# FoX heads of a hybrid decoder: reciprocal row sums on the outputs, by way of DRAM, instead of on the probabilities

## The chip, the cores and the metric

The kernel runs on one core of a Trainium2 chip. The metric is device time in microseconds (us) of one execution, the median of several runs; lower is better. Engines in the profile: PE is TensorE (PEld its weight loads), DVE is VectorE, ACT is ScalarE, POOL is GpSimd, SP is SyncE, which issues most of the transfers.

## The reference

Two layers, each a feed-forward half step, a token mixer and a second feed-forward half step, for 512 tokens of width 1024 in float32. The mixer has 8 forgetting-attention (FoX) heads of width 64 and 4 differential heads. What matters here are the FoX heads:

```
s_f = einsum('bhqd,bhkd->bhqk', qf, k_f) * scale_f
s_f = s_f + cf[..., :, None] - cum_f[..., None, :]
s_f = where(causal, s_f, -inf)
p_f = softmax(s_f, axis=-1)
o_f = einsum('bhqk,bhkd->bhqd', p_f, v_f)
...
return concatenate([o_f, o_d], axis=-1) @ w_out
```

Softmax divides each row of exponentials by its sum. That factor depends on the query alone, so it may stand on the probabilities or on the output `o_f`.

## The kernel before

Every float32 matrix product is made from parts: an operand is split into a rounded high part (ACT) and the rest (DVE), and each product is two or three matmuls (`mm3`, L392 to L394). Weights stream from DRAM into `raw` tiles (issued by SP at L101) and are split into `wg` tiles; L83 and L84 are the two halves of a split, wherever it is called.

In the mixer the twelve heads are units 0 to 11, four differential and then eight FoX heads, and each has four query blocks of 128 rows. A loop over steps does, at step s, the softmax of block s mod 4 of unit s div 4 (`softmax_step`), the transposes of the probabilities of a unit about five steps earlier (`trans_step`, L878, evicted and split at L887 and L888), and the product with the values one step after that (`pv_step`, L917 and L918 for FoX). Between them `fill_to` puts other matmuls, by a table of targets: input projections, gates, values, and the early part of the output projection (`out_early`). When that filler runs short the FoX steps follow each other closely. `out_rest` finishes the output projection: it loads and splits the last block of W_out (rows 3 of eight, L1022) into tile G3, and its matmuls need the output of the last FoX pair.

This is the order in which the code asks for work. The framework under it then orders each engine's instructions by its own estimate of when they can start, and puts in the waits; each engine, and each queue of transfers, then runs strictly in that order.

A FoX block: scores into PSUM; L864 on DVE adds the forget term and finds the row's extreme; L866 on ACT takes the exponential in place and sums the row; L867 on DVE takes the reciprocal of the sum (128x1); L868 on ACT multiplies the block by it. The outputs of two heads are stacked as 128 rows (64 per head) by 512 queries in `fo["u"]` (L947 on ACT, L948 on DVE), and `split_o` (L899, L900) splits that for the output projection.

Probabilities, the pair's output and the rows' tiles lie in two tiles `pg` of 2048 columns, one for even and one for odd units. They occupy the buffers G3 and G4, which before and after the mixer hold weights:

```
pg = [home(f"G{3 + i}", [P, 2048], F32, f"pg{i}") for i in range(2)]
PR = {3: 0, 2: 512, 1: 896, 0: 1152}
...
def pm_tile():
    return pg[nxt("pm", 2)][:, 1280:1792]
```

The forget term of a head comes the same way as the new factors will: `cum_d` in DRAM is read back broadcast over all partitions (L861).

Of the kernel before, what the change touches and what calls it, by code (L numbers as in the profile page):

```python
# [8 lines left out]
F32 = mybir.dt.float32  # L9
F32R = mybir.dt.float32r  # L10
BF16 = mybir.dt.bfloat16
AF = mybir.ActivationFunctionType
ALU = mybir.AluOpType
AX = mybir.AxisListType

P = 128
S = 512
# [5 lines left out]
FOX_H = 8  # L23
DIFF_H = 4
NB = S // P
# [22 lines left out]
def rf(t):  # L48
    return t.bitcast(F32)
# [3 lines left out]
def trunk(ctx, tc, xT, x, gains, gain_row, w_gu, w_dn, w_in, w_ff, w_out, fbias, lams, subln, consts, rope, out):  # L53
    nc = tc.nc
    act, dve, pool, pe, sp = nc.scalar, nc.vector, nc.gpsimd, nc.tensor, nc.sync
# [3 lines left out]
    sm = ctx.enter_context(tc.tile_pool(name="sm", bufs=4))  # L59
    ps = ctx.enter_context(tc.tile_pool(name="ps", bufs=1, space=bass.MemoryType.PSUM))  # L60
    dram = ctx.enter_context(tc.tile_pool(name="dram", bufs=2, space=bass.MemoryType.DRAM))
# [7 lines left out]
    def psum(tag, name=None):  # L69
        return ps.tile([P, S], F32, tag=tag, name=name or f"ps_{tag}", bufs=3 if tag == "a" else 5)  # L70

    def home(tag, shape, dt, name):
        return sb.tile(shape, dt, tag=tag, name=name, bufs=1)

    def t_tile(shape, dt, name, i=None):
        return home(f"t{nxt('t', 6) if i is None else i}", shape, dt, name)
# [143 lines left out]
    for n in range(2 * DEPTH):  # L220
        l = n // 2
        if n % 2 == 1:
            for i in range(24 + len(OUT_K)):
                k = OUT_K[i - 24] if i >= 24 else None
                tag = MIX[i % 3] if i < 24 else None if k >= 4 else MIX[(i - 28) % 3]
# [361 lines left out]
    def mixer(l, n_next, mid):  # L587
# [11 lines left out]
        pg = [home(f"G{3 + i}", [P, 2048], F32, f"pg{i}") for i in range(2)]  # L599
        PR = {3: 0, 2: 512, 1: 896, 0: 1152}  # L600

        def pr_tile(u, qb):
            w = (qb + 1) * P
            return pg[u % 2][:, PR[qb]:PR[qb] + w]

        def pm_tile():
            return pg[nxt("pm", 2)][:, 1280:1792]

        def pair():
            t = home(f"s{nxt('pair', 3)}", [P, 2, S], F32R, "pair")  # L610
            return t[:, 0], t[:, 1]
# [3 lines left out]
        def y_pair(i):  # L615
            return ys[i // 4][:, i % 4], ys[i // 4][:, 4 + i % 4]
# [206 lines left out]
        def scores(q1, kk, m, qb, masked):  # L823
            n = (qb + 1) * P
            w = max(n, 256)
            p = psum("b")
            lq = q1[m][:, qb * P:n]
            pe.matmul(p[:, 0:w], lq, kk[m][:, 0, 0:w], start=True, stop=False)
            pe.matmul(p[:, 0:w], lq, kk[m][:, 1, 0:w], start=False, stop=not masked)
            if masked:  # L830
                pe.matmul(p[:, qb * P:n], identb, maskb, start=False, stop=True)
            return p

        cbs = {}

        def softmax_step(u, qb):
            kind, h = units[u]
            n = (qb + 1) * P
            st = sm.tile([P, 6], F32, tag="st", name="st", bufs=6)
            if kind == "d":  # L840
                q1, kk = qk[("d", h)]
                pm = []
                for m in range(2):
                    p = scores(q1, kk, m, qb, False)
                    e = pr_tile(u, qb) if m == 0 else pm_tile()
                    dve.tensor_tensor_reduce(out=e[:, 0:n], in0=p[:, 0:n], in1=maskw[:, S - n:S], op0=ALU.add,
                                             op1=ALU.min, scale=1.0, scalar=3.0e38, accum_out=st[:, m:m + 1])
                    act.activation(out=e[:, 0:n], in_=e[:, 0:n], func=AF.Exp, scale=-1.0, bias=st[:, m:m + 1],
                                   accum_out=st[:, 2 + m:3 + m])
                    pm.append(e)  # L850
                dve.reciprocal(out=st[:, 4:6], in_=st[:, 2:4])
                dve.tensor_tensor(out=st[:, 5:6], in0=st[:, 5:6], in1=nlam, op=ALU.mult)
                act.mul(out=pm[1][:, 0:n], in_=pm[1][:, 0:n], mul=st[:, 5:6])
                dve.scalar_tensor_tensor(out=pm[0], in0=pm[0], scalar=st[:, 4:5], in1=pm[1][:, 0:n],
                                         op0=ALU.mult, op1=ALU.add)
                probs[u].append(pm[0])
            else:
                q1, kk = qk[("f", h // 2)]
                if qb == 0:
                    cbs[h] = rope_t[h % 2]  # L860
                    sp.dma_start(out=cbs[h], in_=cum_d[h:h + 1, :].partition_broadcast(P))  # L861
                p = scores(q1, kk, h % 2, qb, True)
                e = pr_tile(u, qb)
                dve.tensor_tensor_reduce(out=e, in0=p[:, 0:n], in1=cbs[h][:, 0:n], op0=ALU.add, op1=ALU.min,  # L864
                                         scale=1.0, scalar=3.0e38, accum_out=st[:, 0:1])
                act.activation(out=e, in_=e, func=AF.Exp, scale=-1.0, bias=st[:, 0:1], accum_out=st[:, 2:3])  # L866
                dve.reciprocal(out=st[:, 4:5], in_=st[:, 2:3])  # L867
                act.mul(out=e, in_=e, mul=st[:, 4:5])  # L868
                probs[u].append(e)

        pts = {}

# [22 lines left out]
        fo = {}  # L895

        def split_o(i, u):
            oh, ol = y_pair(i)
            act.copy(out=oh, in_=u)  # L899
            dve.tensor_tensor(out=ol, in0=u, in1=rf(oh), op=ALU.subtract)  # L900
            ovt[i] = (oh, ol)

        def pv_step(u, kb):
            kind, h = units[u]
            if kb == 0:
                po_[u] = psum("b")
            po = po_[u]
            th, tl, cols = pts.pop((u, kb))
            hs = slice(h * P, (h + 1) * P)
            if kind == "d":  # L910
                vh, vl = vd[kb]
                pe.matmul(po[:, cols], vh[:, hs], th, start=kb == 0, stop=False)
                pe.matmul(po[:, cols], vl[:, hs], th, start=False, stop=False)
                pe.matmul(po[:, cols], vh[:, hs], tl, start=False, stop=kb == NB - 1)
            else:
                v = vf[kb][:, hs]
                pe.matmul(po[:, cols], v, th, start=kb == 0, stop=False)  # L917
                pe.matmul(po[:, cols], v, tl, start=False, stop=kb == NB - 1)  # L918
            if kb < NB - 1:
                return  # L920
            po_.pop(u)
            if kind == "d":
                o = os_[h // 2][:, h % 2]
                act.copy(out=o, in_=po)
                sq = t_tile([P, S], F32, "osq")
                act.activation(out=sq, in_=po, func=AF.Square)
                sh_, sl_ = pair()
                act.copy(out=sh_, in_=sq)
                dve.tensor_tensor(out=sl_, in0=sq, in1=rf(sh_), op=ALU.subtract)
                ov[h] = o  # L930

                def stats():
                    pq = psum("b")
                    pe.matmul(pq[0:32], ones[:, 0:32], sh_, start=True, stop=False)
                    pe.matmul(pq[0:32], ones[:, 0:32], sl_, start=False, stop=True)
                    act.activation(out=vv[32 * h:32 * h + 32], in_=pq[0:32], func=AF.Identity, scale=1.0 / P,
                                   bias=eps_t[0:32])
                    if h == DIFF_H - 1:
                        diff_norm()
                later.append(stats)  # L940
            else:
                if h % 2 == 0:
                    fo["u"] = pm_tile()
                own = slice(64 * (h % 2), 64 * (h % 2) + 64)
                oth = slice(64 - 64 * (h % 2), P - 64 * (h % 2))
                t = t_tile([P, S], F32, "fot")
                act.copy(out=t[own], in_=po[oth])  # L947
                dve.tensor_tensor(out=fo["u"][own], in0=po[own], in1=t[own], op=ALU.add)  # L948
                if h % 2 == 1:
                    split_o(h // 2, fo["u"])  # L950

        later = []
# [135 lines left out]
        for s in range(4 * len(units) + 5 + LAG):  # L1088
            u, i = divmod(s, 4)

            def pace(j):
                a = target[min(u, len(target) - 1)]
                b = target[min(u + 1, len(target) - 1)]
                fill_to(a + (b - a) * (3 * i + j) / 12)
            now, later[:] = list(later[:1]), later[1:]
            v, kb = divmod(s - 4 - LAG, 4)
            if 0 <= v < len(units):
                trans_step(v, kb)
            pace(1)
            if u < len(units):  # L1100
                softmax_step(u, i)
            pace(2)
            for f in now:
                f()
            v, kb = divmod(s - 5 - LAG, 4)
            if 0 <= v < len(units):
                pv_step(v, kb)
            pace(3)
# [250 lines left out]
```

## Time and profile before

| | |
|---|---|
| median of 3 runs | 1883.84 us (1880.58 to 1884.79) |
| profiled execution, its own time | 1882.77 us |
| its span, first to last instruction | 1880.5 us |
| mean granted TensorE clock | 0.992 |
| FoX softmax, layer 0 and layer 1 | about 481 to 578 us and 1405 to 1503 us |
| feed-forward after the mixer of layer 0, first matmul | 616.11 us |

How to read the lines further on. The page gives, for each engine, busy us, share of the span and instructions. A row of a stretch gives start and end, its length, then for each engine busy us and the number of instructions, then the granted TensorE clock, the busy share of the 16 transfer engines and GB/s. A row with ACT or DVE alone counts only one source line, named in the text. A row of waits reads: engine, tile and line that waited, `<-` what ended the wait, us in total, times, longest. A row of instructions in time reads: start, duration, engine, line, operation, output `<-` inputs, shape, and in brackets the idle time before it with what ended it. A row of groups gives busy us and mean ns of one. A row of transfers ends with the size and the median us from issue to landing.

### The profile page before, as it was taken

Reading aid. Unit: us, or ns where it says so; the run is one execution under the profiler, and the core shown is the slowest. Engines: PE = TensorE matmul, PEld = TensorE weight load, DVE = VectorE, ACT = ScalarE, POOL = GpSimd, SP = SyncE. Lnnn points to the kernel's source line nnn. Section 1 sums busy time; section 2 is a strip of 40 time slices with the busy share of each in tenths; the row PEclk is TensorE's granted clock in tenths of the full one; section 3 lists DMA queues with packets and bytes.
Section 4 is the critical chain, followed back from the end, with each engine's and each line's share of the span. In section 5 each row is a group of like instructions: output and inputs, shape, how many; then the busy total and the mean of one; then the engine's idle time right before and its main releaser. Section 6 shows DMA issues by size and latency. Waiting matters only on the chain.

```text
span 1880.5 us, 24723 instructions
## 1 busy us (share of the span) xinstructions
PE 1837.3 (98%) x8814; PEld 1511.3 (80%) x8814; DVE 1626.0 (86%) x2538; ACT 1139.3 (61%) x1797; POOL 131.1 (7%) x155
## 2 busy tenths in 40 slices
PE   8999999999999999999999999999999999999997
PEld 6788888787877889888878988887788788888886
DVE  8799989878685989899998989997786869998988
ACT  6565546556785755565485555555577957455564
POOL 2001000000000000001001001000000000000101
PEclk8999999999999999999999999999999999999999
DMA  9677675144336676676647667643333367757842
GB/s 303 190 202 196 166 198 157 59 133 122 94 108 190 182 197 175 162 209 186 169 145 208 183 168 190 169 132 112 112 112 103 111 176 195 208 150 186 223 113 89
DMA packets 95818, 304.86 MB, mean 162 GB/s; under 512 B 12600, under 2 KB 15160, under 8 KB 95696
## 3 DMA queue, kind: packets, MB, share of 16 engines
q1 hardware_dynamic: 74960, 232.68, 36.7%
q0 software_dynamic: 19440, 68.69, 20.8%
q10 hardware_dynamic: 1296, 1.93, 0.3%
q8 instruction: 69, 1.13, 0.2%
q14 instruction: 53, 0.43, 0.1%
HBM read 288.50 MB, written 2.16 MB: 155 GB/s over the span
## 4 chain that ended last, share of the span: by engine, by line
PE 82%; DVE 10%; ACT 5%; DMA 2%; issue 1%; SPq 0%; DVEq 0%; ACTq 0%
PE ps_c L392 12%; PE ps_c L393 12%; PE ps_c L394 12%; PE ps L394 9%; PE ps L392 9%; PE ps L393 9%; PE ps_a L392 3%; PE ps_a L393 3%; PE ps_a L394 3%; DVE wg L84 2%; PE ps_t L494 2%; DVE x L523 1%; ACT pg L866 1%; PE ps_b L878 1%; ACT wg L83 1%
## 5 line engine op out<-in xcount | busy, mean ns | idle before, releaser
L83 ACT CAST wg<-raw 128x1024 fp32r<-128x1024 f32 (+1 forms) x533 | 545.2, 1030 | 490.6 <-PE ps_c L394 183.0
L84 DVE TENSOR_TENSOR wg<-raw,wg 128x1024 fp32r<-128x1024 f32 (+1 forms) x533 | 628.4, 1189 | 111.2 <-ACT wg L83 109.5
L392 PE MATMUL ps_c<-wg,xf 128*128 128x512 f32 (+1 forms) x768 | 288.2, 376 | 4.1 <-ACT wg L83 2.6
L393 PE MATMUL ps_c<-wg,xf 128*128 128x512 f32 (+1 forms) x768 | 287.0, 374 | 1.0 <-DVE wg L84 1.0
L394 PE MATMUL ps_c<-wg,xf 128*128 128x512 f32 (+1 forms) x768 | 285.4, 374 | 0.3 <-DVE xf L84 0.3
L392 PE MATMUL ps<-wg,xf 128*128 128x512 f32 (+1 forms) x576 | 218.3, 380 | 4.9 <-ACT wg L83 3.3
L393 PE MATMUL ps<-wg,xf 128*128 128x512 f32 (+1 forms) x576 | 215.6, 375 | 0.0
L394 PE MATMUL ps<-wg,xf 128*128 128x512 f32 (+1 forms) x576 | 214.8, 375 | 0.2 <-DVE xf L84 0.2
L392 PEld LDWEIGHTS ps_c<-wg,xf 128*128 128x128 f32 x768 | 145.7, 190 | 32.4 <-ACT wg L83 3.2
L393 PEld LDWEIGHTS ps_c<-wg,xf 128*128 128x128 f32 x768 | 146.1, 190 | 26.6 <-DVE wg L84 1.5
L394 PEld LDWEIGHTS ps_c<-wg,xf 128*128 128x128 f32 x768 | 145.2, 190 | 26.1 <-DVE xf L84 0.9
L138 POOL DMA_DIRECT2D raw<-w_gu x87 | 75.5, 867 | 1131.8 <-DMA raw<-w_gu 659.4
L392 PE MATMUL ps_c<-wg,hf 128*128 128x512 f32 x352 | 138.5, 394 | 4.1 <-DVE x L523 4.0
L393 PE MATMUL ps_c<-wg,hf 128*128 128x512 f32 x352 | 137.4, 390 | 0.0
L394 PE MATMUL ps_c<-wg,hf 128*128 128x512 f32 x352 | 137.2, 390 | 0.0
L392 PEld LDWEIGHTS ps<-wg,xf 128*128 128x128 f32 x576 | 109.5, 190 | 23.6 <-ACT wg L83 3.8
L394 PEld LDWEIGHTS ps<-wg,xf 128*128 128x128 f32 x576 | 109.6, 191 | 19.5 <-DVE xf L84 0.5
L523 DVE SCALAR_TENSOR_TENSOR x<-ps_c,x 128x512 f32<-128x512 f32 x192 | 123.9, 680 | 1.0 <-PE ps_c L394 0.9
L393 PEld LDWEIGHTS ps<-wg,xf 128*128 128x128 f32 x576 | 110.0, 191 | 17.9 <-DVE wg L84 0.2
L392 PE MATMUL ps_a<-XA,wg 128*128 128x512 f32 x256 | 106.3, 415 | 3.0 <-ACT XA L346 1.9
L393 PE MATMUL ps_a<-XA,wg 128*128 128x512 f32 x256 | 101.1, 395 | 2.6 <-DVE XA L347 2.5
L393 PE MATMUL ps<-wg,hf 128*128 128x512 f32 x264 | 103.1, 391 | 0.0
(275 smaller groups left out, 3517.3 us busy)
## 6 DMA issues: line engine op xcount, KB each, us to landing
raw<-w_gu SPq DMA_DIRECT2D x219, 512.0 KB, 4.3
raw<-w_dn SPq DMA_DIRECT2D x100, 512.0 KB, 4.0
raw<-w_gu POOLq DMA_DIRECT2D x87, 512.0 KB, 6.8
raw<-w_in SPq DMA_DIRECT2D x48, 512.0 KB, 3.4
raw<-w_dn POOLq DMA_DIRECT2D x40, 512.0 KB, 5.6
kdup<-qk_t SPq DMA_DIRECT2D x64, 128.0 KB, 2.3
raw<-w_out SPq DMA_DIRECT2D x16, 512.0 KB, 3.6
raw<-w_dn SPq DMA_DIRECT2D x20, 256.0 KB, 3.3
```

What stands on the lines that cost most here:

```text
L83: act.copy(out=hi, in_=src)
L84: dve.tensor_tensor(out=lo, in0=src, in1=rf(hi), op=ALU.subtract)
L138: pool.dma_start(out=t, in_=where(two, h)[1], accum_op=ALU.add)
L392: pe.matmul(p, lh, rh, start=start, stop=False, skip_group_check=again)
L393: pe.matmul(p, lh, rl, start=False, stop=False, skip_group_check=again)
L394: pe.matmul(p, ll, rh, start=False, stop=stop, skip_group_check=again)
L494: pe.transpose(pj[j][:, e * 256 + p * P:e * 256 + (p + 1) * P], hs[j][p][:, o:o + P], ident)
L523: dve.scalar_tensor_tensor(out=xc, in0=src, scalar=scale, in1=xc, op0=ALU.mult, op1=ALU.add)
L866: act.activation(out=e, in_=e, func=AF.Exp, scale=-1.0, bias=st[:, 0:1], accum_out=st[:, 2:3])
L878: pe.transpose(p[:, (qb - kb) * P:(qb - kb + 1) * P], probs[u][qb][:, kb * P:(kb + 1) * P], ident)
```

## The change

L867 and L868 go. The exponential writes its row sums into a tile `fs` (128 rows by 4 blocks) for the head; after the fourth block one reciprocal works on 128x4, and SP stores it as 512 numbers of four bytes in DRAM (`rs_d`). When the product with the values of a pair's second head begins, SP reads both heads' rows back, broadcast over 64 partitions each, as two halves of 256 columns into columns 1792 to 2047 of the two `pg` tiles. After L948 of the second head, DVE multiplies each half of the pair's output by it, before `split_o`.

```
+        sums_ = {}
+        rs_d = dram.tile([FOX_H, S], F32, name="rs_d")
+        rb_h = [t[:, 1792:2048] for t in pg]
...
-                act.activation(out=e, in_=e, func=AF.Exp, scale=-1.0, bias=st[:, 0:1], accum_out=st[:, 2:3])
-                dve.reciprocal(out=st[:, 4:5], in_=st[:, 2:3])
-                act.mul(out=e, in_=e, mul=st[:, 4:5])
+                if qb == 0:
+                    sums_[h] = sm.tile([P, NB], F32, tag="fsum", name="fsum", bufs=2)
+                fs = sums_[h]
+                act.activation(out=e, in_=e, func=AF.Exp, scale=-1.0, bias=st[:, 0:1], accum_out=fs[:, qb:qb + 1])
                 probs[u].append(e)
+                if qb == NB - 1:
+                    dve.reciprocal(out=fs, in_=fs)
+                    sp.dma_start(out=rs_d[h].rearrange("(q p) -> p q", p=P), in_=fs)
...
                 po_[u] = psum("b")
+                if kind == "f" and h % 2 == 1:
+                    for i in range(2):
+                        for c in range(2):
+                            sp.dma_start(out=rb_h[c][64 * i:64 * i + 64],
+                                         in_=rs_d[h - 1 + i:h + i, c * 256:c * 256 + 256].partition_broadcast(64))
...
                 if h % 2 == 1:
+                    for c in range(2):
+                        uc = fo["u"][:, c * 256:c * 256 + 256]
+                        dve.tensor_tensor(out=uc, in0=uc, in1=rb_h[c], op=ALU.mult)
                     split_o(h // 2, fo["u"])
```

Line numbers of the changed kernel are higher by 4 up to the softmax (L864 becomes L868, L866 L873), by 8 at the transposes (L878 becomes L886, L887 L895, L888 L896, L899 L907, L900 L908), and by 13 or 16 behind them (L947 becomes L960, L948 L961, L1022 L1038). L83, L84 and L101 keep theirs. New are L876 (reciprocal), L877 (store), L918 (loads) and L965 (multiplication).

The order of instructions moves with it. On ACT, the softmax of unit 10 in layer 0, in the stretch where filler is short; before:

```order
L868 ACTIVATE pg_2961<-pg_2961,st 128x128 [waits DVE_49]
L866 ACTIVATE pg_2961,st<-pg_2961,st 128x256
L947 COPY fot<-ps_b 64x512
L868 ACTIVATE pg_2961<-pg_2961,st 128x256 [waits DVE_49]
L887 CAST pair<-ps_b 128x384 [waits PE_49]
L866 ACTIVATE pg_2961,st<-pg_2961,st 128x384
L887 CAST pair<-ps_b 128x256 [waits PE_49]
L866 ACTIVATE pg_2961,st<-pg_2961,st 128x512 [waits DVE_49]
L868 ACTIVATE pg_2961<-pg_2961,st 128x384 [waits DVE_49]
L887 CAST pt_0_103<-ps_b 128x128 [waits PE_49]
L868 ACTIVATE pg_2961<-pg_2961,st 128x512 [waits DVE_49]
```

and now:

```order
L873 ACTIVATE pg_2961,fsum<-pg_2961,st 128x128 [waits DMAHW2_49,DVE_49]
L895 CAST pair<-ps_b 128x512 [waits PE_49]
L873 ACTIVATE pg_2961,fsum<-pg_2961,st 128x256 [waits DVE_49]
L960 COPY fot<-ps_b 64x512
L895 CAST pair<-ps_b 128x384 [waits PE_49,Activation_49]
L873 ACTIVATE pg_2961,fsum<-pg_2961,st 128x384 [waits DVE_49]
L895 CAST pair<-ps_b 128x256 [waits PE_49,Activation_49]
L895 CAST pt_0_103<-ps_b 128x128 [waits PE_49,Activation_49]
L83 CAST wg<-raw 128x1024 [waits DMAHW2_49]
L873 ACTIVATE pg_2961,fsum<-pg_2961,st 128x512 [waits DVE_49]
```

The four multiplications are gone, and the split of a W_out block has moved in front of the last exponential.

On SP, the end of the mixer of layer 0, where the last head's sums are stored and the last pair's rows are read back (waits named DMAHW are for earlier transfers); now, where before only loads of w_out and w_gu stood:

```order
L877 DMA rs_d<-fsum 128x4x1 [waits DMAHW7_49,DVE_49]
L1038 DMA raw<-w_out 128x1024 [waits DMAHW0_49,DVE_49]
L918 DMA pg_2961<-rs_d 64x256 [waits DMAHW7_49,DMAHW1_49,DVE_49]
L918 DMA pg_2962<-rs_d 64x256 [waits DMAHW2_49,DVE_49]
L101 DMA raw<-w_gu 128x1024 [waits DVE_49]
L101 DMA raw<-w_gu 128x1024 [waits DMAHW4_49,DVE_49]
L877 DMA rs_d<-fsum 128x4x1 [waits DMAHW5_49,DVE_49]
L101 DMA raw<-w_gu 128x1024 [waits DMAHW6_49]
L101 DMA raw<-w_gu 128x1024 [waits PE_49]
L918 DMA pg_2961<-rs_d 64x256 [waits DMAHW5_49,DMAHW0_49]
L918 DMA pg_2962<-rs_d 64x256 [waits DMAHW1_49]
L101 DMA raw<-w_gu 128x1024 [waits DMAHW2_49,PE_49]
```

The last two loads of `rs_d` stand behind the store of unit 11 and behind two prefetches for the next feed-forward, one of which waits for TensorE (the first value product of unit 11), and the first of them waits for the store to land.

On DVE, the same place, from the split of a W_out block to the split of the last pair's output; before:

```order
L888 TENSOR_TENSOR pair<-ps_b,pair 128x512 [waits Activation_49]
L84 TENSOR_TENSOR wg<-raw,wg 128x1024 [waits DMAHW6_49,DVE_49,Activation_49]
L948 TENSOR_TENSOR pg_2962<-ps_b,fot 64x512 [waits Activation_49]
L888 TENSOR_TENSOR pair<-ps_b,pair 128x384 [waits Activation_49]
L888 TENSOR_TENSOR pair<-ps_b,pair 128x256 [waits DVE_49,Activation_49]
L888 TENSOR_TENSOR pt_1_104<-ps_b,pt_0_103 128x128 [waits Activation_49]
L948 TENSOR_TENSOR pg_2962<-ps_b,fot 64x512 [waits Activation_49]
L900 TENSOR_TENSOR y_2963<-pg_2962,y_2963 128x512 [waits Activation_49]
```

and now:

```order
L896 TENSOR_TENSOR pair<-ps_b,pair 128x512 [waits Activation_49]
L961 TENSOR_TENSOR pg_2962<-ps_b,fot 64x512 [waits Activation_49]
L896 TENSOR_TENSOR pair<-ps_b,pair 128x384 [waits Activation_49]
L896 TENSOR_TENSOR pair<-ps_b,pair 128x256 [waits DVE_49,Activation_49]
L896 TENSOR_TENSOR pt_1_104<-ps_b,pt_0_103 128x128 [waits Activation_49]
L961 TENSOR_TENSOR pg_2962<-ps_b,fot 64x512 [waits Activation_49]
L965 TENSOR_TENSOR pg_2962<-pg_2962,pg_2961 128x256 [waits DMAHW1_49,DMAHW0_49,DVE_49]
L965 TENSOR_TENSOR pg_2962<-pg_2962 128x256 [waits DMAHW2_49,DMAHW1_49]
L84 TENSOR_TENSOR wg<-raw,wg 128x1024 [waits Activation_49]
L908 TENSOR_TENSOR y_2963<-pg_2962,y_2963 128x512 [waits Activation_49]
```

The split of the last W_out block (`wg`) has moved from ahead of the last two outputs to behind the two multiplications, and those wait for the transfers.

## Prediction

> **What bounds the kernel now.** I read the page first: span, busy shares, and the chain that ended last.
>
> ```profile
> span 1880.5 us, 24723 instructions
> PE 1837.3 (98%) x8814; PEld 1511.3 (80%) x8814; DVE 1626.0 (86%) x2538; ACT 1139.3 (61%) x1797; POOL 131.1 (7%) x155
> PE 82%; DVE 10%; ACT 5%; DMA 2%; issue 1%; SPq 0%; DVEq 0%; ACTq 0%
> ```
>
> TensorE sets the time of the whole. An edit to ACT and DVE can pay only where TensorE waits for them, so I took busy time by stretch, in and around the FoX heads of both layers.
>
> ```profile
> core 0: us, PE busy (x) PEld busy (x) DVE busy (x) ACT busy (x) POOL busy (x), PEclk, DMA share, GB/s
> 500.00:520.00 20.00, 20.00 (x98) 16.08 (x98) 12.46 (x24) 13.88 (x26) 0.00 (x0) 1.00 0.36 106
> 530.00:540.00 10.00, 10.00 (x53) 7.88 (x52) 9.22 (x23) 7.08 (x17) 0.00 (x0) 1.00 0.42 105
> 540.00:575.00 35.00, 31.58 (x173) 23.42 (x173) 30.38 (x87) 34.52 (x87) 0.00 (x0) 1.00 0.31 91
> 575.00:600.00 25.00, 24.63 (x118) 20.22 (x117) 13.68 (x22) 11.91 (x22) 3.45 (x4) 1.00 0.94 290
> 1464.00:1500.00 36.00, 32.98 (x175) 24.84 (x175) 30.66 (x88) 35.11 (x87) 0.00 (x0) 0.95 0.30 92
> ```
>
> Before 540 us TensorE is full and ACT has a third of its time free. From 540 to 575, and in layer 1 from 1464 to 1500, few other matmuls are left between the FoX steps; there ACT is busy 34.52 of 35 us, and TensorE is not full. The chain through this stretch, and TensorE's waits in it:
>
> ```profile
> by line: ACT pg L866 17.0%; ACT pg L868 15.3%; ACT pair L887 9.2%; ACT fot L947 5.8%; ACT qk L777 4.4%; PE ps_a L392 3.8%; PE ps_a L393 3.6%; DVE y L900 3.4%; DVE pair L888 3.4%; DVE XA L84 3.1%; DVE pg L864 2.9%; ACT qk L765 2.9%; PE ps_a
> PE ps_b L917 <- ACT pair L887: 1.7, 2, 0.9
> PE ps_b L878 <- ACT pg L868: 1.0, 1, 1.0
> PE ps_b L918 <- DVE pair L888: 0.3, 1, 0.3
> ```
>
> The chain runs along ACT, and the second line on it, L868, is the multiplication that the change takes out. So here, and only here, removed ACT work is time.
>
> **The change part by part.** *L868 and L867 go* (64 each). In the two stretches they cost:
>
> ```profile
> core 0: us, ACT busy (x), PEclk, DMA share, GB/s
> 540.00:575.00 35.00, 9.44 (x18) 1.00 0.31 91
> 1464.00:1500.00 36.00, 9.80 (x18) 0.95 0.30 92
> core 0: us, DVE busy (x), PEclk, DMA share, GB/s
> 540.00:575.00 35.00, 2.87 (x18) 1.00 0.31 91
> ```
>
> The other 28 of each lie where TensorE is full (500 to 520: 20.00 of 20) and count nothing. ACT's load of the first stretch falls to 34.52 - 9.44 = 25.1 us. What bounds it next? The new DVE work is sixteen 128x256 multiplications and sixteen 128x4 reciprocals in all, priced by
>
> ```profile
> L888 DVE TENSOR_TENSOR pair<-ps_b,pair 128x256 fp32r<-128x256 f32 x10 | 4.1, 414 | 1.4 <-ACT pair L887 1.4
> L867 DVE RECIPROCAL st<-st 128x1 f32<-128x1 f32 x32 | 5.1, 160 | 4.4 <-ACT pg L866 4.0
> ```
>
> Three head pairs and four heads finish in the stretch: 6 x 0.41 + 4 x 0.17 = 3.1 us against the 2.87 removed, so DVE stays at 30.38 + 0.3 = 30.7. TensorE's own need I take from its weight loads: 23.42 us of them at the density of a full stretch, 16.08 / 20 = 0.804, is 29.1 us. (By its busy time it is 31.58 us.) DVE is next in line. It cannot do better than 30.7 us, a gain of 4.3; at the share it had while TensorE was full (9.22 of 10, 530 to 540) it needs 33.3, a gain of 1.7. Layer 1: 30.9 us of 36, so 5.1 and 2.4. I take 2.8 us per layer, nearer to the lower ends, because DVE still takes turns with ACT and TensorE on each block: **-5.6 us**, ends -9.4 and -4.1. If the cover fails altogether, it is 0.
>
> The Trainium skill, Perfetto Trace Analysis, section Identifying the Most-Contended Engine, says that matmul busy time is a poor measure of TensorE's headroom and weight-load busy time a better one. By the busy row the headroom is 3.4 us per layer, which would cap the sum near 1876; by the load row it is 5.9 and caps nothing.
>
> *The multiplications elsewhere* (the fourth pair, two per layer) and *the 16 stores and 32 loads on SP* run beside other work, unless something waits. Each DVE multiplication waits for its loads, and DVE's queue stands behind it, so I went through the four pairs. For the first three, some ten microseconds of DVE work or more lie between the last reciprocal of the pair and its multiplication in the new order, against about 6 for the round trip priced below; nothing waits. The fourth pair is the tail of the mixer:
>
> ```profile
> 577.18 0.15 DVE L867 RECIPROCAL st<-st 128x1 f32<-128x1 f32 x1
> 577.53 1.23 DVE L84 TENSOR_TENSOR wg<-raw,wg 128x1024 fp32r<-128x1024 f32 x1 [0.19 <-ACT wg L83]
> 580.77 1.05 ACT L83 CAST wg<-raw 128x1024 fp32r<-128x1024 f32 x1
> 582.50 0.94 SPq L101 DMA_DIRECT2D raw<-w_gu  x2
> 586.45 0.70 DVE L948 TENSOR_TENSOR pg<-ps_b,fot 64x512 f32<-64x512 f32 x1 [1.68 <-ACT fot L947]
> 587.18 0.62 ACT L899 CAST y<-pg 128x512 fp32r<-128x512 f32 x1 [0.76 <-DVE pg L948]
> 589.73 0.39 PE L392 MATMUL ps_a<-wg,y 128*128 128x512 f32 x1
> 616.11 0.39 PE L392 MATMUL ps_c<-wg,xf 128*128 128x512 f32 x1
> ```
>
> Before, the last output is whole at 587.15, its cast is done at 587.80, and TensorE takes it up at 589.73. Now two multiplications (0.82) come between. Also the row factors lie in pg, so the last W_out block can go into G3 only after the first multiplication: 587.15 + 0.41 + 1.05 (ACT) + 1.23 (DVE) = 589.84 for its low part, and the output's cast, behind it on ACT, ends at 589.23. TensorE wants them at 589.73 and one matmul (0.23) later, 589.96. That just fits; I charge 0.2 per layer for handovers, **+0.4 us**.
>
> That holds if the factors have landed by 587.2. Rows for the round trip:
>
> ```profile
> SPq L962 <- DMA v_d<-bb: 1.9, 1, 1.9
> kdup<-qk_t SPq DMA_DIRECT2D x8, 128.0 KB, 2.9
> raw<-w_out SPq DMA_DIRECT2D x5, 512.0 KB, 3.6
> raw<-w_gu SPq DMA_DIRECT2D x10, 512.0 KB, 10.7
> ```
>
> A store of 512 single numbers is in no row; the nearest small store took 1.9 us. Bounds: 1.9, and 3.6 as for a whole weight block; I take 2.3, near the small one, since it moves 2 KB. Then the issues of one store and two loads (0.47 each, by 0.94 for two at 582.50) and a load at 2.9: 1.4 + 2.3 + 2.9 = 6.6 us, or 10.2 with the two 512 KB prefetches that stand ahead on SP (1.8 us each at 290 GB/s). Time available: 10.0 us by the rows above (577.18 to 587.15), but in the new order I count only some 9.5 us of TensorE work from the last scores to the last product; with 3.5 to the reciprocal and 1.4 from the product to the whole output that leaves 7.4. So the wait is 0 to 2.8 us per layer. I take 0: one of the prefetches waits on TensorE itself and so starts late. SP's queue behind the loads holds only prefetches for the next feed-forward, first used at 616.11, 29 us on: nothing.
>
> Sum, against the profiled execution's own 1882.77 us: -5.6 + 0.4 = 1877.6. The median of the runs, 1883.84, is 1.07 above it, within their spread; I say **1878 us**.
>
> **Rivals.** *DVE takes ACT's place at once.* For it: DVE is already at 30.4 of 35 us and loses nothing. Against: its idle time in the stretch ends with ACT, not with TensorE. Price: a gain of 0 to 1 us per layer, about 1882.
>
> *Both engines close up to their floors.* For it: the round trip ACT-DVE-ACT is gone from every block, which shortens the path to the transposes. Then -9.4 us, about 1873.5.
>
> *The read-back comes late (slower).* At the tail the transfers are dense (0.94 busy, 290 GB/s), and the prefetches issued there land after 10.7 us instead of 3.6. If the loads queue like them, the round trip is 1.4 + 2.3 + 10.7 = 14.4 us against 7.4: DVE holds at the multiplication, the last W_out block and output behind it, and TensorE 7.0 us per layer. 1882.77 - 5.6 + 14.0 = 1891. It decides from a wait of 2.8 us per layer on. Against it: the dense time begins with the issues after 585, later than these loads. The Trainium skill, DMA: Bandwidth & Descriptors, section Latency and other measured facts, puts memory access at 0.2 us on average and 2 us under high load, the main part of a transfer's fixed cost; that would push towards this rival, and no row here separates it from queueing.
>
> **How the numbers follow.** Forecast 0.52 (its own range 1874 to 1880.5), DVE at once 0.20, floors 0.13, late read-back 0.15. About 0.2% (3.8 us) is what can be told from no change: faster means below 1880.1, slower above 1887.6. Faster: 0.48 of the forecast and 0.13 make 0.61. Same: 0.03 + 0.19 + 0.03 = 0.25. Slower: 0.14, nearly all late read-back. The range leaves out the far part of the late read-back and the best of the floors: 1871 to 1886.5.
>
> **What the next profile would show.** Right: ACT in the stretch near 25 us of 32, the chain there passing to DVE and TensorE, TensorE's waits on the exponentials' line gone, and no wait of DVE for pg<-rs_d above a few tenths. Wrong if the stretch keeps its 35 us with DVE near full (first rival), or if TensorE stands before the last out-projection matmuls while DVE waits for the last rs_d loads (third).

## The result and the profile after

| | kernel before | changed kernel |
|---|---|---|
| median of 4 runs each, same chip | 1883.26 us (1880.58 to 1884.79) | 1967.07 us (1965.12 to 1970.12) |
| ratio, 95% interval | | 1.0445 (1.0430 to 1.0460): slower |
| profiled execution, its span | 1882.77, 1880.5 us | 1968.21, 1966.4 us |

The forecast was 1878 us. The page of the changed kernel, span, busy time and the chain by engine:

```profile
span 1966.4 us, 24754 instructions
PE 1858.5 (95%) x8814; PEld 1527.8 (78%) x8814; DVE 1626.3 (83%) x2506; ACT 1113.9 (57%) x1733; POOL 129.9 (7%) x155
PE 75%; DVE 10%; DMA 9%; ACT 3%; issue 1%; SPq 1%; DVEq 0%; ACTq 0%
```

ACT lost 25.4 us of work and DVE kept its own, as the diff says. But transfers, 2% of the chain before, are now 9%. TensorE stands idle for 1966.4 - 1858.5 = 107.9 us, where it was 43.2, and the same matmuls keep it busy for 21.2 us more. 64.7 + 21.2 is the whole difference of the spans.

By stretches of the changed kernel in layer 0 (columns as before):

```profile
480.00:520.00 40.00, 40.00 (x198) 32.30 (x198) 24.44 (x49) 25.28 (x47) 0.00 (x0) 1.00 0.29 90
520.00:632.00 112.00, 76.00 (x352) 60.19 (x350) 56.67 (x138) 48.47 (x112) 0.86 (x1) 0.84 0.58 98
```

Up to 520 us TensorE is full. From 520 to 632 it has 36 us of gaps, the granted clock is 0.84, and no engine is near its limit. What ends the gaps is on the chain there (start, length, what):

```profile
525.77 12.57 DMA rbd<-ms_d
...
543.39 7.57 DMA kdup<-qk_t
...
558.35 11.46 DMA raw<-w_out
...
572.86 9.28 DMA kdup<-qk_t
...
588.80 8.55 DMA rs_d<-fsum
...
598.55 11.52 DMA raw<-w_out
...
615.04 9.57 DMA rs_d<-fsum
624.67 4.69 DMA pg<-rs_d
629.44 0.43 DVE pg L965
...
630.85 0.62 ACT y L907
```

Only three of these eight transfers belong to the change, 22.8 of their 75.2 us. The other five were there before and now land late. The last cast of a pair's output, at 587.18 us before, is at 630.85: 43.7 us later, and layer 1 adds about as much. The rows of transfers from 475 to 640 us (last column: median us to landing), SP's costliest wait there (us in all, times, longest), and the landing of all stores (min, median, max):

```profile
raw<-w_out SPq DMA_DIRECT2D x8, 512.0 KB, 11.1
kdup<-qk_t SPq DMA_DIRECT2D x12, 128.0 KB, 7.7
rs_d<-fsum SPq DMA_DIRECT2D x8, 2.0 KB, 9.4
SPq L918 <- DMA rs_d<-fsum: 59.9, 8, 10.1
DMA to landing us min/median/max: 7.2/8.9/10.3
```

The store of 2 KB takes 8.9 us, more than the 3.6 us that half a megabyte of W_out took before. W_out's own blocks went from 3.6 to 11.1 us, `kdup` from 2.9 to 7.7. What SP issued shows why it is these (start, length of the issue). Four of the five late ones on the chain are the next thing that SP issued after a store; the fourth is `kdup` at 572.86, behind a store at 572.44. The fifth, W_out's block at 598.55, was issued just ahead of a store, so standing behind one in the queue is not all of it.

```profile
524.78 0.38 SPq L877 DMA_DIRECT2D rs_d<-fsum  x1
525.27 1.39 SPq L986 DMA_DIRECT2D rbd<-ms_d  x3
...
542.29 0.37 SPq L877 DMA_DIRECT2D rs_d<-fsum  x1
542.87 2.40 SPq L776 DMA_DIRECT2D kdup<-qk_t  x4
...
556.49 0.38 SPq L877 DMA_DIRECT2D rs_d<-fsum  x1
558.35 0.33 SPq L101 DMA_DIRECT2D raw<-w_out  x1
...
598.55 0.54 SPq L101 DMA_DIRECT2D raw<-w_out  x1
599.18 0.38 SPq L877 DMA_DIRECT2D rs_d<-fsum  x1
```

### The profile page after: what moved, and what is told of

Read it like the earlier page. It is cut to its first block, busy times and chain, and to the rows that moved or that the text cites. A ratio compares the mean times of both kernels' runs of the same rounds, so it can differ in the third digit from the quotient of the medians.

```text
span 1966.4 us, 24754 instructions
## 1 busy us (share of the span) xinstructions
PE 1858.5 (95%) x8814; PEld 1527.8 (78%) x8814; DVE 1626.3 (83%) x2506; ACT 1113.9 (57%) x1733; POOL 129.9 (7%) x155
## 4 chain that ended last, share of the span: by engine, by line
PE 75%; DVE 10%; DMA 9%; ACT 3%; issue 1%; SPq 1%; DVEq 0%; ACTq 0%
PE ps_c L392 11%; PE ps_c L393 11%; PE ps_c L394 11%; PE ps L394 8%; PE ps L393 8%; PE ps L392 8%; PE ps_a L392 3%; PE ps_a L393 3%; PE ps_a L394 3%; DVE wg L84 3%; DMA raw<-w_out 2%; DMA kdup<-qk_t 2%; DMA rs_d<-fsum 2%; PE ps_t L494 2%; DVE x L523 1%
## 5 line engine op out<-in xcount | busy, mean ns | idle before, releaser
L83 ACT CAST wg<-raw 128x1024 fp32r<-128x1024 f32 (+1 forms) x533 | 545.2, 1030 | 524.8 <-PE ps_c L394 186.3
L84 DVE TENSOR_TENSOR wg<-raw,wg 128x1024 fp32r<-128x1024 f32 (+1 forms) x533 | 628.7, 1189 | 109.7 <-ACT wg L83 106.5
L392 PE MATMUL ps_a<-XA,wg 128*128 128x512 f32 x256 | 108.5, 424 | 2.4 <-ACT XA L346 1.9
L393 PE MATMUL ps_a<-XA,wg 128*128 128x512 f32 x256 | 103.4, 404 | 2.6 <-DVE XA L347 2.5
L394 PE MATMUL ps_a<-XA,wg 128*128 128x512 f32 x256 | 103.1, 403 | 0.0
```

The source lines that it names most:

```text
L83: act.copy(out=hi, in_=src)
L84: dve.tensor_tensor(out=lo, in0=src, in1=rf(hi), op=ALU.subtract)
L392: pe.matmul(p, lh, rh, start=start, stop=False, skip_group_check=again)
L393: pe.matmul(p, lh, rl, start=False, stop=False, skip_group_check=again)
L394: pe.matmul(p, ll, rh, start=False, stop=stop, skip_group_check=again)
```

## The experiments

Three theories stood at the start. Theory 1: the element-wise store holds up transfers for some 9 us, eight times per layer. Theory 2: SP runs in order and waits for the store to land before the loads, 59.9 us per layer, and cannot issue anything meanwhile. Theory 3: the new order of instructions, with DVE's multiplications ahead of the split of the output, causes the loss. Where only one run was made, no interval is given.

### Whose loss it is

**Without the transfers.**

```
+        for t in rb_h:
+            pool.memset(t, 0.01)
...
-                    sp.dma_start(out=rs_d[h].rearrange("(q p) -> p q", p=P), in_=fs)
...
-                            sp.dma_start(out=rb_h[c][64 * i:64 * i + 64],
-                                         in_=rs_d[h - 1 + i:h + i, c * 256:c * 256 + 256].partition_broadcast(64))
```

> The changed kernel without the stores and the loads of the row factors: the factors are one constant, set once per layer, so the outputs of the FoX heads are scaled by 0.01 and not by the reciprocal sums. All arithmetic of the change stays (no multiplication of the blocks on ACT, sums in fsum, reciprocal 128x4, two multiplications per pair on DVE), and so does the new order of the instructions. Theory 1, the element-wise store holds up its transfer queue (8.9 us to land, eight per layer): the whole loss goes, and what is left is the relief of ACT, -5.6 us against the kernel before by the prediction's term, 1874 to 1881 us. Theory 2, SP waits in order for the store to land before it can issue anything else (60 us per layer): the same time. Theory 3, the new order and the DVE multiplications ahead of the output's split cause the loss: 1930 us or more.

Measured: 1874.64 us, ratio 0.9938 (0.9925 to 0.9952). Theory 3 falls: with all its arithmetic and its order, but without its transfers, the change is a gain. The two stretches of the prediction in this kernel:

```profile
540.00:575.00 35.00, 33.88 (x188) 26.48 (x187) 32.65 (x82) 29.54 (x70) 0.00 (x0) 1.00 0.39 117
1464.00:1500.00 36.00, 34.88 (x199) 27.66 (x199) 33.30 (x81) 29.88 (x72) 0.00 (x0) 1.00 0.42 133
```

ACT has gone from 34.52 to 29.54 us there, and TensorE from 31.58 to 33.88: the relief of ACT works.

**The transfers alone,** added to the kernel before:

```
-                dve.reciprocal(out=st[:, 4:5], in_=st[:, 2:3])
-                act.mul(out=e, in_=e, mul=st[:, 4:5])
+                dve.reciprocal(out=fs[:, qb:qb + 1], in_=st[:, 2:3])
+                act.mul(out=e, in_=e, mul=fs[:, qb:qb + 1])
...
+                    sp.dma_start(out=rs_d[h].rearrange("(q p) -> p q", p=P), in_=fs)
...
+                            sp.dma_start(out=rb_h[c][64 * i:64 * i + 64],
+                                         in_=rs_d[h - 1 + i:h + i, c * 256:c * 256 + 256].partition_broadcast(64))
```

> The kernel before with all its arithmetic (reciprocal 128x1 and the multiplication of each block on ACT), but the reciprocals are kept in a tile, stored as 512 numbers of 4 bytes per head, and read back as in the change; nobody uses what is read back. Theories 1 and 2 (the loss is the transfers'): some 84 us of loss plus the 5.6 us of relief that this kernel does not have, so 1960 to 1975 us. Theory 3 (order and DVE multiplications): 1883 to 1890 us.

Measured: 1965.21 us (one run), 80 above the kernel before. The loss is the transfers', and nothing has to wait for the factors themselves.

**The stores alone.** The run without transfers, with the stores put back.

> The changed kernel with the sixteen stores, but without the loads; the factors are one constant, as in the run without transfers. SP then has nothing that waits for a store to land. Theory 1 (transfers issued behind a store on the same queue land late, SP's wait or not): most of the loss stays, 1935 to 1965 us, and kdup<-qk_t and raw<-w_out still land in 7 us or more. Theory 2 (SP's wait for the landing is the loss): 1876 to 1890 us, and kdup lands in 3 us.

Measured: 1958.48 us (one run). Nothing on SP waits for a store any more, yet 84 of the 92 us between the run without transfers and the changed kernel are there. Theory 2 falls as the main cause. From 475 to 640 us, `kdup` lands even later than in the changed kernel (10.0 against 7.7 us), and W_out's blocks at 7.6, between the 3.6 of the kernel before and the 11.1 of the changed one:

```profile
raw<-w_out SPq DMA_DIRECT2D x8, 512.0 KB, 7.6
kdup<-qk_t SPq DMA_DIRECT2D x12, 128.0 KB, 10.0
rbd<-ms_d SPq DMA_DIRECT2D x4, 256.0 KB, 12.6
```

**The store on another queue.**

```
-                    sp.dma_start(out=rs_d[h].rearrange("(q p) -> p q", p=P), in_=fs)
+                    act.dma_start(out=rs_d[h].rearrange("(q p) -> p q", p=P), in_=fs)
```

> The changed kernel, complete, with the store issued by ACT on its own queue and the loads still by SP. Theory 1 in the form that the store holds only its own queue: kdup<-qk_t and raw<-w_out that do not stand behind the loads land in about 3 to 4 us again; SP still waits for the store's landing at the loads, so the time falls to 1890 to 1930 us. Theory 1 in the form that the store holds the transfer engines whatever the queue: all transfers stay late, 1950 to 1970 us. Theory 2 (SP's wait): no change, 1960 to 1970 us, though kdup lands early.

Measured: 1976.08 us (one run), above every expectation, and no better. Transfers in the stretch, then three stores as ACT issued them, and three pieces of the chain:

```profile
kdup<-qk_t SPq DMA_DIRECT2D x12, 128.0 KB, 3.7
rs_d<-fsum ACTq DMA_DIRECT2D x8, 2.0 KB, 9.3
```
```profile
556.75 0.37 ACTq L877 DMA_DIRECT2D rs_d<-fsum  x1
...
573.89 0.37 ACTq L877 DMA_DIRECT2D rs_d<-fsum  x1
...
589.63 0.37 ACTq L877 DMA_DIRECT2D rs_d<-fsum  x1
```
```profile
558.69 12.58 DMA raw<-w_out
...
575.32 12.28 DMA raw<-w_out
...
590.77 12.75 DMA raw<-w_out
```

In the median `kdup` is nearly as early as before. But four copies that SP issued at 542.92, 0.5 us after a store began on ACT's queue, still stand on the chain with 7.86 us, and each of the three blocks of W_out shown here was issued by SP 1.1 to 1.9 us after such a store, and landed 12.3 to 12.8 us later. So the store does not only stand ahead of them in a queue; it slows the transfers of the other queue too. This agrees with the Trainium skill, DMA: Bandwidth & Descriptors, section Issuing engines are not separate DMA queues: what different engines issue runs on the same 16 transfer engines and interleaves there.

### What makes the store slow

The first reading was the number of its pieces (1a). It was tested against the smallness of the writes (1b), then against closeness (1c: pieces that lie close together in DRAM wait for each other) and 4 bytes as such (1d).

**16-byte pieces.**

```
-                    sp.dma_start(out=rs_d[h].rearrange("(q p) -> p q", p=P), in_=fs)
+                    sp.dma_start(out=rs_d[h].rearrange("(p q) -> p q", q=NB), in_=fs)
```

> The changed kernel, complete, with one edit: the store writes the four sums of a row side by side, 128 pieces of 16 bytes instead of 512 of 4 (so the factors stand in another order than the columns that they multiply, with the same work everywhere). Theory 1a, the store costs by the number of its pieces: from 512 pieces in 8.9 us and 1.9 us for one piece (v_d<-bb), 128 pieces land in 1.9 + 7.0 / 4 = 3.7 us, and the time falls to 1880 to 1900 us. Theory 1b, any store in pieces far under a row costs the same by its small writes, whatever their number: still 7 us or more, and 1940 us or more.

Measured: 1881.32 us, ratio 0.9978 (0.9968 to 0.9988). One line takes 86 us off, and the store lands in 2.4 us:

```profile
kdup<-qk_t SPq DMA_DIRECT2D x12, 128.0 KB, 2.3
rs_d<-fsum SPq DMA_DIRECT2D x8, 2.0 KB, 2.4
```

That fitted 1a. The next run did not.

**128 pieces of 4 bytes,** side by side: stores only, `out=rs_d[h].rearrange("(q p) -> p q", p=P)[:, 0:1], in_=fs[:, 0:1]`. (The expectation has their distance wrong; the one after it says so.)

> As the run with stores only (no loads, constant factors), but each store writes only the first of the four columns: 128 pieces of 4 bytes, 512 bytes apart in DRAM. Theory 1a, number of pieces: it costs what 128 pieces of 16 bytes cost; kdup<-qk_t lands in 3 to 5 us and the time is 1878 to 1895 us, 65 to 80 us under that with 512 pieces. Theory 1b, size and distance of the pieces: near the 1958 us of the store with 512.

Measured: 1933.91 us (one run), the store 8.0 us. A quarter of the pieces and of the bytes cost nearly the same. 1a falls.

**The same, 64 and 16 bytes apart:** `out=rs_d[h].rearrange("(p q) -> p q", p=P)[:, 0:1]`, with rows of `rs_d` of 2048 and of 512 numbers.

> As the last run with stores only (no loads, constant factors, 128 pieces of 4 bytes), but each piece goes to a place of its own, 64 bytes from the next. The expectation of that run called its pieces 512 bytes apart in DRAM; they lay side by side, 4 bytes apart, and cost 8.0 us a store, when 128 pieces of 16 bytes, also side by side, had cost 2.4. Theory 1c, small writes into the same stretch of memory wait for each other: with 64 bytes between them the store lands in 2 to 3 us, kdup<-qk_t in 2.5 to 3 us, and the time is 1874 to 1880 us. Theory 1d, a piece of 4 bytes is slow wherever it goes: 8 us again, kdup in 7 us or more, and 1925 to 1940 us.

> The same with the pieces of 4 bytes 16 bytes apart, at the places where the fast store put its pieces of 16 bytes. Theory 1c, the same stretch of memory: if the stretch is 64 bytes or more, four pieces share one as in the fast store, so 2 to 4 us and 1874 to 1885 us. Theory 1d, the size of the piece: 8 us and 1925 to 1940 us.

Measured: 1872.61 and 1876.07 us (one run each). 1d falls: pieces of 4 bytes cost nothing that shows when they lie 16 or 64 bytes apart.

**All 512 pieces, 16 bytes apart; and 128 pieces, 8 bytes apart:** the same edit, with `"(q p z) -> p q z", p=P, z=4` and with rows of 256 numbers.

> Stores only (no loads, constant factors), all 512 pieces of 4 bytes, but each 16 bytes from the next in DRAM. Theory 1c, only pieces that lie close together wait for each other: kdup<-qk_t lands in 2.3 to 3 us and the time is 1872 to 1880 us, as with 128 such pieces (1876.1). Theory 1a, the number of pieces matters too: between that and the 1958.5 us of 512 pieces side by side; if number alone made the difference of 512 and 128 side by side (1958.5 and 1933.9), then about 1890 to 1900 us.

> Stores only, 128 pieces of 4 bytes, 8 bytes apart. Between 4 bytes apart (1933.9 us, kdup in 7.5 us) and 16 apart (1876.1 us, 2.4 us). Theory 1c with a wait that grows with the pieces in a stretch of 64 bytes (16, 8 and 4 of them): about half of the 8.0 us, so 4 to 5 us, and 1885 to 1910 us. If instead what counts is whether a piece has 8 bytes (or 16) to itself: as fast as 16 apart, 1872 to 1880 us (or as slow as 4 apart, 1925 to 1940 us).

Measured: 1877.89 and 1889.15 us (one run each). All runs with stores only:

| pieces of one store | distance in DRAM | to landing, us | time, us |
|---|---|---|---|
| 512 of 4 bytes | 4 bytes | 10.7 | 1958.48 |
| 128 of 4 bytes | 4 bytes | 8.0 | 1933.91 |
| 128 of 4 bytes | 8 bytes | 5.7 | 1889.15 |
| 128 of 4 bytes | 16 bytes | 2.0 | 1876.07 |
| 128 of 4 bytes | 64 bytes | 3.2 | 1872.61 |
| 512 of 4 bytes | 16 bytes | 3.9 | 1877.89 |
| no store | | | 1874.64 |

(A landing is seen only where something waits for it, and here each is that of one store; the times carry the argument.) Distance decides: with 512 pieces, 4 bytes against 16 bytes between them is 80 us; with 128 it is 58. The number adds some when they are close, next to nothing when they are not. Here is the packet count of the two kernels with 512 pieces, side by side and 16 bytes apart, and of the one without stores:

```profile
DMA packets 104267, 304.90 MB, mean 156 GB/s; under 512 B 21048, under 2 KB 23608, under 8 KB 104144
DMA packets 104267, 304.90 MB, mean 163 GB/s; under 512 B 21048, under 2 KB 23608, under 8 KB 104144
DMA packets 95819, 304.86 MB, mean 163 GB/s; under 512 B 12601, under 2 KB 15161, under 8 KB 95697
```

The first two agree to the last packet, and are 80 us apart. The Trainium skill, DMA: Bandwidth & Descriptors, Specifications, says that a transfer under 512 bytes is done by reading, changing and writing back. That could make neighbours wait for one another, but this is a guess: the runs here show only the effect of the distance, not what causes it. By size alone the fast stores, as far under 512 bytes, should be slow too. Between 16 and 64 bytes no limit of the stretch was found, and 16-byte pieces side by side are fast as well, so several of them may share 64 bytes.

### What is left for the change

**Rows before the store.** TensorE transposes the sums to 4x128, DVE takes the reciprocal from there, SP stores four rows of 512 bytes.

```
-                    dve.reciprocal(out=fs, in_=fs)
-                    sp.dma_start(out=rs_d[h].rearrange("(q p) -> p q", p=P), in_=fs)
+                    p4 = psum("b")
+                    pe.transpose(p4[0:NB, 0:P], fs, ident)
+                    dve.reciprocal(out=fr, in_=p4[0:NB, 0:P])
+                    sp.dma_start(out=rs_d[h].rearrange("(q p) -> q p", p=P), in_=fr)
```

> The changed kernel, complete, with the sums turned into rows before they are stored: TensorE transposes the tile of sums (128x4 to 4x128 in PSUM), DVE takes the reciprocal from there into a row tile of 4x128, and SP stores 4 pieces of 512 bytes. Theory 1: the store lands in about 2 us like v_d<-bb, nothing else is late, and the relief of ACT comes out: 1874 to 1882 us, faster than the kernel before; the added 16 small transposes cost under 0.3 us each. Theory 2 (SP's wait for the landing is what counts): SP still waits some 2 us per load pair, about 1885 to 1895 us.

Measured: 1885.51 us, ratio 1.0006 (0.9998 to 1.0015). The loss is gone, but so is the gain. The time is the one given for theory 2, but not its reason: SP waits 6.7 us in layer 0 for these stores, and 10.6 in the faster form below. The reciprocal, the first stretch, and SP's wait here and there:

```profile
L879 DVE RECIPROCAL frow<-ps_b x16: 935/939/946, 497.1 to 1507.8; 4x128 f32<-4x128 f32 x16
540.00:575.00 35.00, 31.00 (x174) 23.58 (x172) 32.82 (x73) 28.14 (x66) 0.00 (x0) 1.00 0.45 131
```
```profile
SPq L921 <- DMA rs_d<-frow: 6.7, 6, 2.9
```
```profile
SPq L918 <- DMA rs_d<-fsum: 10.6, 5, 3.2
```

The reciprocal of 4x128 takes 0.94 us where 128x4 took 0.17. DVE is as busy there as without transfers (32.82 against 32.65), but TensorE does 2.9 us less. That the longer reciprocal is the cause was not tested by itself.

**16-byte pieces, read in their order.** The complete, usable form of the fast store, called the repaired kernel from here on.

```
+                        uc = fo["u"].rearrange("m (q c p) -> m c q p", q=NB, c=2)[:, c]
+                        rc = rb_h[c].rearrange("m (p q) -> m q p", q=NB)
+                        dve.tensor_tensor(out=uc, in0=uc, in1=rc, op=ALU.mult)
```

> The changed kernel, complete, with the store of 128 pieces of 16 bytes and a multiplication on DVE that reads the factors in the order in which they then lie (every fourth number). If the strided reading costs DVE nothing: the 1881 us of the store in 16 byte pieces, 0.2% under the kernel before. If it makes the 128x256 multiplication slower (0.41 us without stride): up to 0.4 us at each of the 16, mostly hidden, 1 us at the tails, so 1881 to 1884.

Measured: 1881.50 us, ratio 0.9984 (0.9975 to 0.9993), faster than before by 0.16%. The strided multiplication takes 0.62 us instead of 0.42. The tail of layer 0 on its chain, and TensorE's wait there over both layers:

```profile
578.21 3.73 DMA rs_d<-fsum
582.00 3.93 DMA pg<-rs_d
586.01 0.62 DVE pg L966
PE ps_a L392 <- ACT y L907: 2.8, 2, 1.9
```

**Loads by POOL.** As the run before, with `pool.dma_start` for the loads.

> As the run before, with the loads issued by POOL instead of SP, so that SP never waits for a store to land (10.2 us per layer with 16 byte pieces). Theory 2, what is left of the gap to the run without transfers (1874.6 us) is SP's wait in order: 1875 to 1879 us. Against it: what is left is the factors' landing at the tail and the issues themselves, which POOL makes slower: 1881 to 1887 us.

Measured: 1888.81 us, ratio 1.0018 (1.0008 to 1.0028): slower than either expectation said. Taking the wait from SP gained nothing in sum, but this does not show that the wait costs nothing: the loads that POOL issues reach the tail later (TensorE's wait for the last pair's output is 6.7 us over both layers, where it was 2.8), and that can hide a gain elsewhere.

**The multiplication on POOL,** in the kernel before: `pool.tensor_scalar(out=e, in0=e, scalar1=st[:, 4:5], scalar2=None, op0=ALU.mult)` for L868.

> The kernel before with the multiplication of each block moved from ACT to POOL, and nothing else: the same relief of ACT as the change has, without any transfer. If the relief is all that is needed: 1872 to 1880 us, like the run without transfers. If POOL takes longer for a block than ACT (0.5 us) the path from the exponential to the transposes grows, and in the stretch without filler TensorE waits for POOL: 1885 to 1900 us.

Measured: 1898.02 us, ratio 1.0074 (1.0059 to 1.0090). POOL takes 1.24 us for a block in the median, ACT took 0.56, and TensorE waits for it:

```profile
PE ps_b L878 <- POOL pg L868: 15.9, 22, 1.7
```

**The last pair as before.** The 16-byte form for three pairs; the last two heads keep reciprocal and multiplication on ACT.

```
+                if h >= FOX_H - 2:
+                    act.activation(out=e, in_=e, func=AF.Exp, scale=-1.0, bias=st[:, 0:1], accum_out=st[:, 2:3])
+                    dve.reciprocal(out=st[:, 4:5], in_=st[:, 2:3])
+                    act.mul(out=e, in_=e, mul=st[:, 4:5])
```

> The repaired kernel (16-byte pieces, factors read in the order in which they lie; 1881.5 us), with the last pair's two heads done as before: reciprocal 128x1 and multiplication of each block on ACT, no store, no loads. If the rest of the gap is the round trip at the tail (3.7 us of store and 3.9 us of load on the chain of layer 0 at 578 us): 1876 to 1879 us. If the relief of ACT in the last two heads is worth as much as the round trip costs: 1880 to 1883 us, no change against the repaired kernel.

Measured: 1876.21 us, ratio 0.9958 (0.9945 to 0.9970). This form leaves nothing out and beats both kernels, by 0.4% and 4.7%. It takes 0.26 of the 0.46% that the repaired kernel lacked of the run without transfers, and its interval reaches that run's, so more than half of what was left was the round trip at the tail.

**One load pair per head,** issued at each head's own product.

> The repaired kernel with each head's rows read back when its own product with the values begins, two loads each time, instead of four at the pair's second head. If the number of loads behind the last store is what makes the tail late (two fewer issues of 0.47 us): 1 to 2 us better, 1879 to 1881 us. If the landing of the last store and load is all: 1881 to 1882 us. If SP's wait for the first head's store now holds up other transfers earlier: 1883 to 1886 us.

Measured: 1878.45 us, ratio 0.9970 (0.9958 to 0.9982). That is about 2 to 3 us better than the repaired kernel, a little more than the two issues were expected to give, but the two intervals overlap (0.9975 is the lower end of the other).

## Why the prediction was wrong, point by point

- **The price of the store: the first step that failed.** The prediction bounded it by 1.9 and 3.6 us and took 2.3 "since it moves 2 KB". It took 8.9. Both bounding rows were of transfers in long runs, one row of 2 KB and rows of 4 KB; neither says anything of pieces of 4 bytes that lie side by side. An upper end from the nearest row in bytes was no upper end. With pieces of 16 bytes, or 16 bytes or more apart, the median landing was 2.0 to 3.9 us, about what the bounds said. But the price alone does not give the loss: in the prediction's own sum, 8.9 makes the round trip 13.2 us, the wait at the tail 5.8 per layer, and the time about 1889.
- **"The 16 stores and 32 loads on SP run beside other work, unless something waits": the larger step that failed.** What the transfers do to other transfers was put at nothing, without a reason; the search went through the waits for the factors only. The runs showed that the store delays the transfers of older work, `kdup`, `rbd` and W_out. The stores alone cost 84 of 92 us, though their landing is waited for only once (2.7 us, by an exponential that reuses the tile of sums). With the loads in place, part of the same time shows as waits for the change's own transfers (22.8 of 75.2 us on the chain above).
- **SP's queue behind the loads:** called free at the tail, where only prefetches follow. At the first three pairs `kdup`, `rbd` and W_out's blocks follow, and the sentence was not asked of them. By the run with the stores alone this wait is not the main cause.
- **The relief of ACT: right in place and direction.** The forecast was -5.6 us; without the transfers the profiled executions differ by 1882.77 - 1876.72 = 6.05, and the medians by 10.6, beyond the end of -9.4. In the two stretches TensorE's gaps fall from 3.42 + 3.02 to 1.12 + 1.12 us (4.2), and the clock of 0.95 in the second becomes 1.00 (an estimate: 0.05 x 36 = 1.8). That this adds up to 6.0 is in part luck: over the whole span TensorE's gaps fell by only 1.9 us (43.2 to 41.3), since others grew, and its busy time by 3.7. Where the medians' further 4.6 us lie, these two profiles do not show.
- **"DVE is next in line": half right.** Without the transfers DVE rose to 32.65 of 35 us and passed ACT, but TensorE, at 33.88, is nearer its end.
- **DVE's prices: right.** 0.42 us for the 128x256 multiplication (0.41 said), 0.17 for the reciprocal.
- **The tail, costed at 0.4 us per kernel and no wait:** too low even with a fast store. The round trip is 3.73 + 3.93 = 7.7 us, over the 7.4 available, and keeping the last pair as before gains about 0.26% (0.9958 against 0.9984), some 5 us.
- **The rivals.** The late read-back had the sign. Its 14.4 us at the tail are what the tail shows (9.57 + 4.69 = 14.3), but that is luck: it came by a slow store and not by dense loads. The reason given against it was misread, too: before the change the transfer engines were 0.74 to 0.87 busy already from 575 to 584 us, not only after 585. It priced 7 us per layer where 44 were lost: it looked at one pair, and at the change's own transfers.

## What to carry to other kernels

Price a transfer by its pieces, and look at how close they lie: numbers from 128 partitions, written side by side one by one, took a median of 8 to 9 us to land here, and four from a partition in one piece 2.4. Then ask of every slow transfer which older transfers run at the same time, since it may delay those more than its own reader; another queue did not help. A factor that takes a round trip through memory may go where something covers it, and not at the last step of a chain.

## What the runs showed of the hardware that was not expected

- Stores of the same packets, bytes and number differ by 80 us of kernel time with the distance of their pieces in DRAM (the table above).
- The busy share of the transfer engines does not show it. In the changed kernel the rows of transfers are nearly empty while a store is under way: from 529 to 535 us with the loads of `rbd` not yet landed, and from 592 to 598 with the store of 588.80 not yet landed (597.35):

```profile
529.00:535.00 6.00, 0.71 (x6) 0.43 (x4) 0.00 (x0) 0.15 (x2) 0.00 (x0) 0.73 0.07 8
592.00:598.00 6.00, 4.25 (x27) 3.39 (x26) 3.02 (x8) 2.07 (x6) 0.00 (x0) 1.00 0.03 3
```

- Where TensorE waited, it was also slower when it worked. Near the tail of the changed kernel (600 to 635 us, granted clock 0.79; before, 1.00 from 589 to 616), a matmul of 512 columns that took 0.39 us before shows min, median and max in ns of

```profile
L392 PE MATMUL ps_a<-wg,y x12: 389/553/792, 600.5 to 634.6; 128*128 128x512 f32 x12
```

That is part of the 21.2 us that TensorE's busy time grew by. That the gaps bring the clock down is read from the two going together; no run here separates them.
